# The modulation's columns for the first norm, summed in four groups of the array side by side instead of two

## The chip, the cores and the metric

The kernel runs on one core of one Trainium2 chip. The metric is the device time of one execution in microseconds (us); lower is better. Five engines work side by side on it: TensorE (PE in the profile, its weight loads PEld), VectorE (DVE), ScalarE (ACT), GpSimd (POOL) and SyncE (SP), which here issues the large transfers.

## What is computed

The reference is a transformer block with adaptive normalisation, sparse attention and a mixture of experts, followed by a second block. The change touches the first lines of the first block: the modulation vector `mod`, of which the first two sixths, the shift `sh1` and the scale `sc1`, go into the first norm.

```python
def first_block(x, c, ada_w, ada_b, ln1_g, ln2_g, w_in, ...):
    cond = jax.nn.silu(c)                                  # (1, 1024)
    for l in range(DEPTH):                                 # DEPTH = 1
        mod = (cond @ ada_w[l] + ada_b[l])[:, None, :]     # (1, 1, 6144)
        sh1, sc1, g1, sh2, sc2, g2 = jnp.split(mod, 6, axis=-1)
        h = rms_norm(x, ln1_g[l]) * (1.0 + sc1) + sh1      # x: (1, 512, 1024)
        x = x + g1 * hybrid_mixer(h, w_in[l], ...)
        ...
```

## The kernel before

512 tokens of width 1024 lie in four tiles of 128 tokens. After the first norm, `h` is needed turned, with its 1024 columns on the partitions in eight pieces `k` of 128, as the stationary operand of the product with `w_in` (`zchunk`, lines 257 to 259: three matmuls for each piece and token tile, since each operand is split in a high and a low part).

`start` makes `h` and begins this product. It works in four steps `jb` of 256 columns of `sc1` and `sh1`, that is of two pieces `k`. In a step, `ada(jb)` multiplies `cond` with two loaded blocks of `ada_w` (q = 0 for the scale, q = 1 for the shift, 8 x 128 rows by 256 columns, 1 MB each). `cond` stands 32 times over as the stationary operand, so a product takes 32 columns of the array and gives 32 equal rows. The products over `k` alternate between two 32-column groups of the array, groups 0 and 1 for q = 0 and groups 2 and 3 for q = 1, and so there are two partial sums for each q. Each of the 16 products of a step shows in the trace as two matmuls, 32 in all (line 468). ScalarE copies the bank to SBUF (line 472), `columns(jb)` turns it with TensorE (line 479) and adds up the two partial sums and the bias on VectorE (lines 483 to 490; the results are `A1` and `B1`, scale and shift by column), and `rows(jb)` turns the tokens (line 497), applies `A1` and `B1` on ScalarE (lines 499 and 500) and takes the low part on VectorE (line 501).

Step 0 runs ahead of the product with `w_in`. Steps 1 to 3 are hooks in it: `ada(jb)` is issued ahead of piece k = 2 jb - 2, `columns(jb)` and `rows(jb)` ahead of the next piece. The order on each engine is that of the code. The blocks are loaded by `Stream.pump` (line 135) on SP in the order in which they are used; they are split in a high part (line 167, ScalarE) and a low part (line 168, VectorE) if they belong to `w_in` or the experts. From 440 us on the weights of 32 experts (384 loads of 1 MB) stream through the same buffers.

Of the kernel before, what the change touches and what calls it, by code (L numbers as in the profile page):

```python
# [14 lines left out]
OP = mybir.AluOpType  # L15
AX = mybir.AxisListType
# [4 lines left out]
T = 512  # L21
NT = 4
D = 1024
KD = 8
# [163 lines left out]
class Build:  # L188
# [245 lines left out]
    def start(self):  # L434

        nc, I, st = self.nc, self.I, self.st
        mm = nc.tensor.matmul
        x = [self.xin[i // 2].v((i % 2) * D, D) for i in range(NT)]
        names = self.names = ["a0", "a1"]
        self.tb = self.sb = self.ring(names)  # L440
        pc = self.tb()
        nc.tensor.transpose(pc[:, :32], self.rows_a, self.ident[:32, :32])
        nc.vector.tensor_copy(self.cola, pc[:, :32])
        self.mb = self.ar.get()
        cond = self.mb.cols(0, 8)
        condr = self.condr = self.mb.v(256, KD, 32)
        nc.scalar.activation(cond, self.cola[:, 0:8], AF.Exp, scale=-1.0)
        nc.vector.tensor_scalar(cond, cond, 1.0, None, op0=OP.add)
        nc.vector.reciprocal(cond, cond)
        nc.vector.tensor_tensor(out=cond, in0=cond, in1=self.cola[:, 0:8], op=OP.mult)  # L450
        nc.vector.tensor_copy(condr, cond[:, :, None].to_broadcast([P, KD, 32]))
        sc = self.ar.get()
        A1, B1 = self.small(8, "A1", 1), self.small(8, "B1", 1)
        self.hT = [self.ar.get(F32R) for _ in range(4)]
        hH, hL = self.views(self.hT[:2]), self.views(self.hT[2:])
        self.hv = (hH, hL)

        sums = {}

        def ada(jb):  # L460

            pa = self.bank("a3")
            for q in range(2):
                u = self.u_ada1[jb][q]
                v = st.view(u)
                for k in range(KD):
                    o = 64 * q + 32 * (k % 2)
                    mm(pa[o:o + 32, 0:256], lhsT=condr[:, k, :], rhs=v[:, k, :], start=(k < 2), stop=(k >= KD - 2),
                       tile_position=(0, o))
                st.free(u)  # L470
            r = sums[jb] = sc.cols(D + 256 * (jb % 2), 256)
            nc.scalar.copy(r, pa[:, 0:256])

        def columns(jb):

            r = sums.pop(jb)
            pb = self.bank("a2")
            for j in range(2):
                nc.tensor.transpose(pb[:, j * P:(j + 1) * P], r[:, j * P:(j + 1) * P], self.ident)
            rows = self.small(8, "ab")  # L480
            p3 = pb[:, 0:256].rearrange("p (j g c) -> p j g c", j=2, g=4)[:, :, :, 0]
            r3 = rows.rearrange("p (j g) -> p j g", j=2)
            nc.vector.tensor_copy(r3, p3)
            s = slice(2 * jb, 2 * jb + 2)
            t = self.small(4, "abt")
            nc.vector.tensor_tensor(out=t[:, 0:2], in0=r3[:, :, 0], in1=r3[:, :, 1], op=OP.add)
            nc.vector.tensor_tensor(out=t[:, 2:4], in0=r3[:, :, 2], in1=r3[:, :, 3], op=OP.add)
            nc.vector.tensor_tensor(out=t[:, 0:2], in0=t[:, 0:2], in1=self.cola[:, 24 + 2 * jb:26 + 2 * jb], op=OP.add)
            nc.vector.tensor_tensor(out=B1[:, s], in0=t[:, 2:4], in1=self.cola[:, 16 + 2 * jb:18 + 2 * jb], op=OP.add)
            nc.vector.scalar_tensor_tensor(A1[:, s], t[:, 0:2], 1.0, self.cola[:, 8 + 2 * jb:10 + 2 * jb], op0=OP.add,  # L490
                                           op1=OP.mult)

        def rows(jb):
            for kk in (2 * jb, 2 * jb + 1):
                px = self.tb()
                for i in range(NT):
                    nc.tensor.transpose(px[:, i * P:(i + 1) * P], x[i][:, kk * P:(kk + 1) * P], self.ident)
                hf = sc.cols((kk % 2) * T, T)
                nc.scalar.activation(hf, px, AF.Identity, bias=B1[:, kk:kk + 1], scale=A1[:, kk:kk + 1])
                nc.scalar.copy(hH(kk), hf)  # L500
                nc.vector.tensor_tensor(out=hL(kk), in0=hf, in1=hH(kk), op=OP.subtract)

        def hook(k):
            jb = k // 2 + 1
            if jb < 4:
                if k % 2 == 0:
                    ada(jb)
                else:
                    columns(jb)
                    rows(jb)  # L510

        ss = self.small(NT, "ss")
        for i in range(NT):
            nc.scalar.activation(sc.cols(0, D), x[i], AF.Square, accum_out=ss[:, i:i + 1])
        nc.vector.tensor_scalar(ss, ss, 1.0 / D, EPS, op0=OP.mult, op1=OP.add)
        ri = self.rsqrt(ss, NT, "ri")
        for i in range(NT):
            if i % 2:
                nc.scalar.mul(x[i], x[i], ri[:, i:i + 1])
            else:  # L520
                nc.vector.tensor_scalar(x[i], x[i], ri[:, i:i + 1], None, op0=OP.mult)
        ada(0)
        columns(0)
        rows(0)

        self.cc = self.ar.get()
        c0, n, ids = self.z_chunks[1]
        self.weave(self.zchunk(self.hv, ids, n, lambda i, ps: self.z_evac(1, i, ps), hook=hook), thunks=0)
        self.ar.put(sc, *self.xin)
# [1904 lines left out]
```

## Time and profile before

| | us |
|---|---|
| median of 3 runs | 1750.85 |
| lowest and highest | 1750.61, 1752.01 |
| profiled execution, its own time | 1751.53 |
| its span in the trace | 1749.8 |
| TensorE busy in it | 1641.9 (94%) |
| VectorE, ScalarE, GpSimd busy | 1100.6, 847.0, 383.4 |
| first matmul of the modulation (line 468) | starts at 12.71 |

How the views read: a row of the timeline has its start, its length (from the first start to the last end), engine, line, operation, what it writes and reads, shapes and how many instructions are merged; in brackets stand the idle time ahead of it and what ended that. A row of the lines view has a group's count, its busy time and the mean ns of one. A row of the windows view has the stretch, its length, the busy time of each engine with the instructions in brackets, then TensorE's granted clock (1.00 is 2.4 GHz, 0.50 is 1.2 GHz), the share of the DMA engines' time and their GB/s. A row of the waits view has the time waited, how often, and the longest. In a merged row the last matmul ends later than it stops feeding the array, since matmuls are pipelined.

### The profile page before, as it was taken

The numbers are of one execution on the slowest core, as the hardware profiler recorded it, in microseconds if no ns is written. First come the engines' busy times: TensorE is split into PE (matmuls) and PEld (weight loads), VectorE is DVE, ScalarE is ACT, GpSimd is POOL, SyncE is SP. The second block draws the span as 40 slices with busy tenths as digits, with TensorE's granted clock in tenths as the row PEclk, the third lists the DMA queues.
The fourth block names the chain that finished last, engine by engine and source line by source line (L and its number), as shares of the span: only waits on it lengthen the run. The fifth ranks groups of instructions, "written<-read, shape, count | busy, mean of one in ns | idle before, by whom it ended". The sixth has DMA issues, their size and how long they took to land. (4 is left out here: it accounts for less than half of the span.)

```text
span 1749.8 us, 22154 instructions
## 1 busy us (share of the span) xinstructions
PE 1641.9 (94%) x7957; PEld 1059.2 (61%) x7958; DVE 1100.6 (63%) x1741; ACT 847.0 (48%) x1321; POOL 383.4 (22%) x259
## 2 busy tenths in 40 slices
PE   6999998898899999999999999999999989999998
PEld 3677764576765664564554454455455446778887
DVE  2567668668875575575475485476476486476653
ACT  4346568525554354264254254245245254477571
POOL 3012225223010120320320321231232130210120
PEclk9999999998999999999999999999999999999999
DMA  9712035456899999999999999999999986100301
GB/s 363 300 52 73 1 135 182 153 224 262 317 365 419 406 416 416 406 415 418 410 415 420 409 418 418 409 417 419 410 417 419 409 353 247 49 25 25 121 1 48
DMA packets 100007, 506.53 MB, mean 289 GB/s; under 512 B 10962, under 2 KB 20258, under 8 KB 48690
## 3 DMA queue, kind: packets, MB, share of 16 engines
q1 hardware_dynamic: 89972, 477.94, 67.1%
q0 software_dynamic: 9296, 26.07, 5.4%
q8 instruction: 64, 1.05, 0.2%
q10 hardware_dynamic: 624, 1.06, 0.2%
q14 instruction: 51, 0.42, 0.1%
HBM read 487.19 MB, written 17.84 MB: 289 GB/s over the span
## 5 line engine op out<-in xcount | busy, mean ns | idle before, releaser
L168 DVE TENSOR_TENSOR b<-b,b 128x1024 fp32r<-128x1024 f32 (+1 forms) x474 | 557.2, 1221 | 266.0 <-ACT b L167 265.3
L167 ACT CAST b<-b 128x1024 fp32r<-128x1024 f32 (+1 forms) x476 | 472.1, 1044 | 205.6 <-DMA b<-in_exp_w 163.5
L1739 POOL DMA_INDIRECT accd<-b,isc x16 | 162.3, 10146 | 431.0 <-DVE b L1734 431.0
L257 PE MATMUL z<-b,b 128*128 128x512 f32 (+1 forms) x544 | 225.0, 414 | 2.9 <-ACT b L167 2.1
L257 PE MATMUL u<-b,b 128*96 128x512 f32 (+1 forms) x560 | 224.7, 401 | 0.0
L259 PE MATMUL u<-b,b 128*96 128x512 f32 (+1 forms) x560 | 220.0, 393 | 0.0
L258 PE MATMUL u<-b,b 128*96 128x512 f32 (+1 forms) x560 | 219.7, 392 | 0.0
L1592 PE MATMUL u<-b,b 128*64 128x512 f32 x960 | 216.8, 597 | 1.4 <-DMA b<-in_exp_w 1.3
L258 PE MATMUL z<-b,b 128*128 128x512 f32 (+1 forms) x544 | 210.7, 387 | 1.5 <-DVE b L168 1.5
L259 PE MATMUL z<-b,b 128*128 128x512 f32 (+1 forms) x544 | 210.4, 387 | 0.0
L1592 PEld LDWEIGHTS u<-b,b 128*64 128x64 f32 x960 | 64.6, 136 | 123.0 <-issue 113.2
L258 PE MATMUL y<-b,b 128*96 128x512 f32 (+1 forms) x256 | 107.6, 420 | 21.0 <-DVE b L168 19.5
L257 PEld LDWEIGHTS z<-b,b 128*128 128x128 f32 x544 | 103.1, 190 | 33.5 <-issue 13.4
L257 PE MATMUL y<-b,b 128*96 128x512 f32 (+1 forms) x256 | 105.3, 411 | 17.5 <-ACT b L167 17.5
L257 PEld LDWEIGHTS u<-b,b 128*96 128x96 f32 (+1 forms) x560 | 96.1, 172 | 37.3 <-ACT b L167 5.7
L259 PEld LDWEIGHTS z<-b,b 128*128 128x128 f32 x544 | 102.7, 189 | 21.8 <-DVE b L1931 0.4
L259 PEld LDWEIGHTS u<-b,b 128*96 128x96 f32 (+1 forms) x560 | 95.8, 171 | 33.0
L258 PEld LDWEIGHTS u<-b,b 128*96 128x96 f32 (+1 forms) x560 | 96.1, 172 | 30.5
L258 PEld LDWEIGHTS z<-b,b 128*128 128x128 f32 x544 | 103.3, 190 | 16.2 <-DVE b L168 2.5
L1611 ACT CAST b<-tr 128x768 fp32r<-128x768 f32 (+1 forms) x33 | 28.6, 867 | 163.9 <-PE tr L1609 163.9
L1592 PE MATMUL y<-b,b 128*64 128x512 f32 x480 | 107.6, 600 | 0.0
L259 PE MATMUL y<-b,b 128*96 128x512 f32 (+1 forms) x256 | 103.5, 404 | 0.0
(516 smaller groups left out, 2101.4 us busy)
## 6 DMA issues: line engine op xcount, KB each, us to landing
b<-in_exp_w SPq DMA_DIRECT2D x384, 1024.0 KB, 19.5
b<-in_ada_w SPq DMA_DIRECT2D x24, 1024.0 KB, 8.8
b<-in_w_in SPq DMA_DIRECT2D x24, 1024.0 KB, 11.5
b<-in_w_out SPq DMA_DIRECT2D x8, 1024.0 KB, 5.2
b<-in_x SPq DMA_DIRECT2D x8, 512.0 KB, 4.3
b<-in_nsa_cmp_w POOLq DMA_DIRECT2D x2, 1024.0 KB, 10.1
b<-modd SPq DMA_DIRECT2D x4, 512.0 KB, 5.5
accd<-b SPq DMA_DIRECT2D x4, 512.0 KB, 3.8
```

What stands on the lines that cost most here:

```text
L167: nc.scalar.copy(hv, s)
L168: (other or nc.vector).tensor_tensor(out=lv, in0=s, in1=hv, op=OP.subtract)
L257: mm(out, lhsT=ah, rhs=bh, start=first, stop=False)
L258: mm(out, lhsT=ah, rhs=bl, start=False, stop=False)
L259: mm(out, lhsT=al, rhs=bh, start=False, stop=last)
L1592: mm(out[o, :], lhsT=lhsT, rhs=rhs[:, h * 512:(h + 1) * 512], start=False, stop=last, tile_position=(0, 64 * h), skip_group_check=True)
L1611: nc.scalar.copy(H[:, :, 0:n], pv)
L1739: nc.gpsimd.indirect_dma_start(out=self.accd, out_offset=bass.IndirectOffsetOnAxis(ap=self.isc[0:m, c:c + 1], axis=0), in_=ys[0:m, :], in_ ...
```

## The change

The product over `k` now goes round all four groups for both q: product `k` takes group `k % 4`, and q picks the columns of the bank (0 to 255 or 256 to 511) instead of the groups. So there are four partial sums of two products each, in place of two of four products each, and the bank holds 512 columns. The copy by ScalarE takes 512 columns, the turn takes four matmuls, and one reduction on VectorE over the four groups replaces a copy and two additions.

```diff
                 for k in range(KD):
-                    o = 64 * q + 32 * (k % 2)
-                    mm(pa[o:o + 32, 0:256], lhsT=condr[:, k, :], rhs=v[:, k, :], start=(k < 2), stop=(k >= KD - 2),
-                       tile_position=(0, o))
+                    o = 32 * (k % 4)
+                    mm(pa[o:o + 32, q * 256:(q + 1) * 256], lhsT=condr[:, k, :], rhs=v[:, k, :], start=(k < 4),
+                       stop=(k >= 4), tile_position=(0, o))
                 st.free(u)
-            r = sums[jb] = sc.cols(D + 256 * (jb % 2), 256)
-            nc.scalar.copy(r, pa[:, 0:256])
+            r = sums[jb] = sc.cols(D + T * (jb % 2), T)
+            nc.scalar.copy(r, pa)
...
-            for j in range(2):
+            for j in range(4):
                 nc.tensor.transpose(pb[:, j * P:(j + 1) * P], r[:, j * P:(j + 1) * P], self.ident)
-            rows = self.small(8, "ab")
-            p3 = pb[:, 0:256].rearrange("p (j g c) -> p j g c", j=2, g=4)[:, :, :, 0]
-            r3 = rows.rearrange("p (j g) -> p j g", j=2)
-            nc.vector.tensor_copy(r3, p3)
             s = slice(2 * jb, 2 * jb + 2)
             t = self.small(4, "abt")
-            nc.vector.tensor_tensor(out=t[:, 0:2], in0=r3[:, :, 0], in1=r3[:, :, 1], op=OP.add)
-            nc.vector.tensor_tensor(out=t[:, 2:4], in0=r3[:, :, 2], in1=r3[:, :, 3], op=OP.add)
+            nc.vector.tensor_reduce(out=t, in_=pb.rearrange("p (j g c) -> p j g c", j=4, g=4)[:, :, :, 0], axis=AX.X,
+                                    op=OP.add)
```

The matmuls of line 468 keep their number and their place. On VectorE, in step 0 (`a` with a number is a bank of PSUM, `abt` the sums), this stood in a row before:

```order
L521 TENSOR_SCALAR b_79<-b_79,riy 128x1024
L483 COPY ab<-a_196 128x8
L486 TENSOR_TENSOR abt<-ab 128x2
L487 TENSOR_TENSOR abt<-ab 128x2
L488 TENSOR_TENSOR abt<-abt,cola 128x2
L489 TENSOR_TENSOR B_151<-abt,cola 128x2
L490 SCALAR_TENSOR_TENSOR A_150<-abt,cola 128x2
L501 TENSOR_TENSOR b_154<-b_149,b_152 128x512 x2
```

Now there are four instructions between the same neighbours instead of six, in this step and in the three after it:

```order
L517 TENSOR_SCALAR b_79<-b_79,riy 128x1024
L482 TENSOR_REDUCE abt<-a_196 128x4
L484 TENSOR_TENSOR abt<-abt,cola 128x2
L485 TENSOR_TENSOR B_151<-abt,cola 128x2
L486 SCALAR_TENSOR_TENSOR A_150<-abt,cola 128x2
L497 TENSOR_TENSOR b_154<-b_149,b_152 128x512 x2
```

On TensorE the stretch from the end of step 0 to the first product with `w_in` read like this before (the lines 497 of before are 493 now):

```order
L468 MATMUL a_174<-b_89,b_143 32x256 x8
L479 MATMUL a_196<-ident,b_149 128x128 x2
L497 MATMUL a_207<-ident,b_78 128x128 x2
L497 MATMUL a_207<-ident,b_79 128x128 x2
L497 MATMUL a_215<-ident,b_78 128x128 x2
L497 MATMUL a_215<-ident,b_79 128x128 x2
L468 MATMUL a_228<-b_93,b_143 32x256 x8
L468 MATMUL a_228<-b_95,b_143 32x256 x8
L257 MATMUL z_224<-b_135,b_152 128x512
```

It now reads:

```order
L468 MATMUL a_174<-b_89,b_143 32x256 x8
L479 MATMUL a_196<-ident,b_149 128x128 x4
L493 MATMUL a_206<-ident,b_78 128x128 x2
L493 MATMUL a_206<-ident,b_79 128x128 x2
L493 MATMUL a_214<-ident,b_78 128x128 x2
L493 MATMUL a_214<-ident,b_79 128x128 x2
L468 MATMUL a_227<-b_93,b_143 32x256 x8
L468 MATMUL a_227<-b_95,b_143 32x256 x8
L257 MATMUL z_223<-b_135,b_152 128x512
```

Nothing has moved but the two matmuls more at line 479; no engine's order differs otherwise.

## Rows read from the trace of the kernel before

**Rows 1.** The page, part 1: busy time of each engine.
```profile
PE 1641.9 (94%) x7957; PEld 1059.2 (61%) x7958; DVE 1100.6 (63%) x1741; ACT 847.0 (48%) x1321; POOL 383.4 (22%) x259
```

**Rows 2.** Windows: the opening, the dense part behind it, the experts.
```profile
12.60:18.80 6.20, 6.02 (x32) 2.60 (x32) 1.33 (x2) 2.12 (x3) 3.16 (x6) 1.00 1.07 376
18.80:29.40 10.60, 5.68 (x44) 3.16 (x44) 3.41 (x10) 5.31 (x8) 0.00 (x0) 1.00 1.08 386
29.40:113.00 83.60, 81.69 (x507) 56.38 (x507) 41.35 (x122) 30.18 (x55) 12.01 (x13) 1.00 0.65 246
...
440.00:1440.00 1000.00, 953.39 (x4253) 546.91 (x4255) 627.54 (x620) 446.90 (x480) 221.34 (x60) 0.99 1.00 407
```

**Rows 3.** Timeline of TensorE, 12 to 42 us.
```profile
12.71 6.02 PE L468 MATMUL a<-b,b 128*32 128x256 f32 x32 [7.87 <-DMA b<-in_ada_w]
...
19.48 1.04 PE L497 MATMUL a<-ident,b 128*128 128x128 f32 x8
22.12 1.92 PE L468 MATMUL a<-b,b 128*32 128x256 f32 x16 [1.60 <-DMA b<-in_ada_w]
24.78 1.92 PE L468 MATMUL a<-b,b 128*32 128x256 f32 x16 [0.74 <-DMA b<-in_ada_w]
28.12 0.50 PE L257 MATMUL z<-b,b 128*128 128x512 f32 x1 [1.42 <-ACT b L167]
29.38 0.50 PE L258 MATMUL z<-b,b 128*128 128x512 f32 x1 [0.76 <-DVE b L168]
...
35.65 0.39 PE L259 MATMUL z<-b,b 128*128 128x512 f32 x1
35.96 2.82 PE L468 MATMUL a<-b,b 128*32 128x256 f32 x32
38.71 0.50 PE L257 MATMUL z<-b,b 128*128 128x512 f32 x1
...
41.57 0.38 PE L479 MATMUL a<-ident,b 128*128 128x128 f32 x2
```

**Rows 4.** Timeline of TensorE's weight loads (PEld) in step 0.
```profile
16.03 0.19 PEld L468 LDWEIGHTS a<-b,b 128*32 128x32 f32 x4 [0.57 <-DMA b<-in_ada_w]
```

**Rows 5.** Lines of TensorE: line 468 in 12.6 to 16, then 22 to 27.
```profile
L468 PE MATMUL a<-b,b 128*32 128x256 f32 x16 | 3.6, 632 | 7.9 <-DMA b<-in_ada_w 7.9
...
L468 PE MATMUL a<-b,b 128*32 128x256 f32 x32 | 3.8, 381 | 2.3 <-DMA b<-in_ada_w 2.3
```

**Rows 6.** Timeline of TensorE at 67.5 us: the four-group form, eight matmuls of 512 columns.
```profile
67.57 1.06 PE L641 MATMUL a<-b,b 128*32 128x512 f32 x8
```

**Rows 7.** Timeline of ScalarE behind step 1.
```profile
26.75 0.37 ACT L472 COPY b<-a 128x256 f32<-128x256 f32 x1 [3.46 <-PE a L468]
27.02 1.99 ACT L167 CAST b<-b 128x1024 fp32r<-128x1024 f32 x2
```

**Rows 8.** Lines of ScalarE, 28 to 140 us, shapes apart.
```profile
L567 ACT COPY b<-z 128x512 f32<-128x512 f32 x4 | 2.3, 586 | 5.8 <-PE z L259 5.7
```

**Rows 9.** Lines of VectorE, 18 to 70 us.
```profile
L588 DVE TENSOR_REDUCE vk<-b 128x8 f32<-128x512 f32 x1 | 0.7, 685 | 0.0
...
L483 DVE COPY ab<-a 128x8 f32<-128x8 f32 x4 | 0.7, 167 | 8.9 <-PE a L479 8.9
```

**Rows 10.** Timeline of TensorE at 445 us.
```profile
444.80 0.63 PE L257 MATMUL u<-b,b 128*128 128x512 f32 x1
445.22 0.63 PE L258 MATMUL u<-b,b 128*128 128x512 f32 x1
```

**Rows 11.** Windows: stretches around changes of the clock.
```profile
442.00:447.70 5.70, 5.50 (x14) 4.00 (x15) 5.04 (x6) 2.94 (x4) 0.00 (x0) 0.50 0.45 178
...
745.00:748.00 3.00, 0.52 (x2) 0.21 (x2) 1.30 (x2) 1.99 (x2) 0.00 (x0) 1.00 1.02 431
748.00:751.50 3.50, 3.50 (x9) 2.76 (x10) 3.41 (x4) 3.42 (x4) 0.00 (x0) 0.51 1.01 426
```

**Rows 12.** Waits of the SP queue, 300 to 440 us.
```profile
SPq L135 <- DVE b L168: 52.4, 9, 30.5
```

## The prediction

> **What bounds the kernel now.** Read the busy times first: TensorE is busy 94% of the span, no other engine over 63% [rows 1]. Then the windows [rows 2]: in the opening (12.6 to 29.4 us) the DMA engines are full (shares 1.07 and 1.08) and TensorE is busy 5.68 of 10.60 us in its second part; from 29.4 to 113 us TensorE is busy 81.69 of 83.60 us with the transfers at 0.65; the experts (440 to 1440 us) have TensorE at 953 of 1000 us and the DMA engines at 1.00. So the change sits where the kernel goes from waiting for loads to being dense on TensorE, and what counts is when the dense part begins and how long it is. The timeline [rows 3] tells how the opening ends: step 0 (12.71) and both blocks of step 1 (22.12 and 24.78) wait for a transfer of `ada_w`; the first product with `w_in` waits for line 167 (28.12) and its second for line 168 (29.38); from there no wait over 0.4 us until steps 2 (35.96) and 3 (the same row, at 45.50) are done. In step 0 the second block comes at 16.03 [rows 4].
>
> One more thing is to be read, TensorE's clock. Its column says 1.00 for the opening [rows 2], but the matmuls of line 468 take 632 ns on the mean from 12.6 to 16 us and 381 ns from 22 us on [rows 5]: the engine starts at the lower level (1.2 GHz) and rises to 2.4 GHz between, after it worked 6.02 of 6.20 us in step 0 [rows 2].
>
> **The change part by part.** *A burst.* Sixteen matmuls of one block take 1.92 us, of which the last is 0.38 [rows 3]: eight in each of two groups, so seven steps in 1.54, 0.22 us a step. Over four groups there are four in each: 3 x 0.22 + 0.38 = 1.04 us, 0.88 less. That four groups do work side by side is in the trace: line 641 does eight matmuls of 512 columns over four groups in 1.06 us, where one after the other on two groups the four steps of 0.44 would take over 1.7 [rows 6]. In steps 2 and 3 both blocks are there, and the 32 matmuls take 2.82 us, since the second block's groups already overlap the first's; eight in each of four groups give 7 x 0.22 + 0.38 = 1.92, 0.90 less in each of the two steps.
>
> *Step 0* gains and loses nothing that lasts: step 1 waits for its transfer at 22.12 whatever step 0 does [rows 3].
>
> *Step 1, the path.* Its second block arrives at 24.78. Before, the burst ends at 26.70, line 472 copies 256 columns in 0.37 us, and line 167 follows at 27.02 [rows 7], ahead of the dense part. A copy of 512 columns by ScalarE takes 0.59 us [rows 8], so +0.21 here. In steps 2 and 3 the longer copy stands between TensorE's burst and work that is needed one piece later, and costs nothing.
>
> *Turns.* Two matmuls more in each of four steps, at (1.04 - 0.27) / 7 = 0.11 us each (0.27 us is the last one's tail, estimated from line 479's row of two, 0.38 - 0.11) [rows 3]; in step 0 they lie before a wait, in steps 1 to 3 on the dense engine: 6 x 0.11 = +0.66.
>
> *VectorE.* A reduction takes the place of a copy and two additions. Nothing shows a reduction of 16 numbers; it lies between the 0.17 us of the copy of eight and the 0.69 of a reduction of 512, and I take 0.2, near the small one [rows 9]. The two further turns hold it up by 0.22, one dependent instruction less gives about 0.2 back, and `A1` and `B1` come as before. Even 0.69 lies beside some 12 products with `w_in` in steps 1 to 3 (35.65 is the last of them) and costs nothing.
>
> So far, at the upper clock: step 1 -0.88 + 0.21, turns +0.66, steps 2 and 3 -1.80, together -1.81 us.
>
> *The clock.* This sum takes the upper clock for granted. At the lower one a matmul takes 0.63 us [rows 5], and a step, at half the rate, 0.44: a four-group burst takes 3 x 0.44 + 0.63 = 1.95 us. Step 0 then runs from 12.71 to 14.66, waits for its second block until 16.03 [rows 4], and ends at 17.98. Before, it had no such gap: at half the array's width the first block lasted until the second came. The changed opening is bursts of 1.95 us and turns of some 2.8 us with waits between them, up to the dense part. Wherever the trace shows the clock going from 0.50 to 1.00, the engine had worked nearly unbroken: 6.02 of 6.20 us [rows 2], 5.50 of 5.70 us from 442.0, 3.50 of 3.50 us from 748.0 [rows 11]. And where it stood idle (0.52 us of work in 745.0 to 748.0) the clock fell right behind [rows 11]. I take it that the clock stays at the lower level until the dense part has run for a while: between 3.5 us (748.0 to 751.5) and 5.7 us (442.0 to 447.7), 4.6 in the middle. A product with `w_in` then takes 0.42 us [rows 10] instead of (41.57 - 38.71) / 12 = 0.24 [rows 3], so 0.18 x 4.6 / 0.42 = +2.0 us, with ends 1.5 and 2.4. Step 1's second burst is 1.95 instead of 1.92, so its -0.88 becomes +0.03.
>
> The Trainium skill bears on this place (TensorE: Matmul & The Clock Gate, "HAM oscillation — how this bites in real kernels"): bursts that are short against the transfer waits between them send the clock down, and the work should be laid so that the engine isn't left idle. That rule speaks against this change, which shortens the bursts and not the waits. By that rule the sum would be the one with the clock's term, without it the -1.81 above.
>
> Sum: +0.03 + 0.21 + 0.66 - 1.80 + 2.0 = **+1.1 us**, from 0.6 to 1.5 by the clock's ends.
>
> *What becomes of it.* From 29.4 us TensorE is dense, so all of it moves on. The first experts' loads wait for buffers that line 168 frees (52.4 us in nine waits of SP) [rows 12], so the transfers that fill 440 to 1440 us begin later by the same amount. I carry it whole; the other end is that the full DMA engines swallow it.
>
> The profiled execution took 1751.53 us, its span 1749.8 and 1.7 around it; with +1.1 it would be 1752.6. It lies 0.7 above the median of the three runs, 1750.85, and against that I forecast **1752.0 us**.
>
> **The rivals.** *The clock rises all the same,* in the turns of step 0 or by what the engine did before the trace begins to show it, and holds as it held before with TensorE busy 5.68 of 10.60 us [rows 2]. For it: that half-idle stretch did keep the upper level. Against: in the changed kernel the same stretch would hold about 10 x 0.11 + 0.27 + 0.22 for the turns, 2 x 1.04 and 0.5, some 4.2 of 10.6 us, and the rise must come first. Then -1.81: 1749.0 us.
>
> *Four groups don't work side by side here,* as all products of a block share one moving block. Then only the costs are left, 0.21 + 0.66 = +0.9: 1751.7. Against it stands line 641, which runs this very form [rows 6].
>
> *Slower, by a lower clock further on.* At 748.0 the engine had waited for lines 167 and 168, the clock fell, and 3.5 us were at 0.51 [rows 11]: at 0.18 of 0.42 us that is 1.5 us lost. Further starts of experts wait in the same way and keep the clock. If the shift by one microsecond brings two or more of them under, that decides it: 1.1 + 2 x 1.5 = +4.1, 1755.0. Against it: in the experts the transfers are full and may hide such a loss [rows 2]. The mirror of it, two such falls less on top of the first rival, gives 1749.0 - 3.0 = 1746.0.
>
> **How the numbers follow.** The forecast has 0.60, the rise all the same 0.22, no overlap 0.04, the further falls 0.08, fewer falls 0.06. A measurement of this kernel can tell about 0.2%, 3.5 us, from no change: under 1747.35 is faster, over 1754.35 slower. Only the last two cases lie outside, so faster 0.06, same 0.86, slower 0.08. For the range: the forecast's own is 1751.4 to 1752.4, with the three runs' spread of 1.4 around it, and the carry's lower end is 1750.85; the first rival is at 1749.0. From 1748.6 to 1753.7 takes in all but the last two cases and edges of the others.
>
> **What would show it.** In step 0 the row of line 468 splits in two with a gap up to 16.03, and line 468's mean is still over 600 ns in step 1, with bursts of 1.95 us; then the clock's step is right. Means near 380 ns there and bursts of 1.04 say the first rival. Line 257 first starts near 28.35; the products behind 29.6 are 0.42 apart until 33 to 35 us and 0.23 after. Steps 2 and 3 are rows of 32 in 1.9 us; 2.8 would say that the groups don't overlap. A dense part that begins 0.7 earlier with the clock up, or an end that doesn't follow the opening's shift, makes the prediction wrong.

## The result, and the profile after

The changed kernel takes **1762.62 us** (median of 4 runs, 1761.52 to 1762.99) against 1751.43 us (median of 4) for the kernel before: ratio 1.0062, 95% interval 1.0050 to 1.0074. It is slower by about 11 us. The forecast was 1752.0 us, and its range ended at 1753.7. The profiled execution of the changed kernel took 1761.52 us, its span is 1759.8.

The busy times answer to [rows 1], part 1 of the page of the kernel after:

```profile
PE 1648.0 (94%) x7965; PEld 1066.5 (61%) x7966; DVE 1101.4 (63%) x1733; ACT 849.3 (48%) x1321; POOL 382.4 (22%) x259
```

They tell nothing of 10 us: ScalarE has 2.3 us more, VectorE 0.8, and TensorE 6.1, which at 94% of a longer span says little.

The opening is told by the timeline of TensorE in the kernel after (columns as in [rows 3]):

```profile
13.48 1.93 PE L468 MATMUL a<-b,b 128*32 128x256 f32 x16 [8.15 <-DMA b<-in_ada_w]
16.46 1.94 PE L468 MATMUL a<-b,b 128*32 128x256 f32 x16 [1.05 <-DMA b<-in_ada_w]
19.10 1.11 PE L479 MATMUL a<-ident,b 128*128 128x128 f32 x4 [0.71 <-ACT b L472]
...
22.40 1.75 PE L468 MATMUL a<-b,b 128*32 128x256 f32 x16 [0.47 <-DMA b<-in_ada_w]
25.32 1.07 PE L468 MATMUL a<-b,b 128*32 128x256 f32 x16 [1.18 <-DMA b<-in_ada_w]
28.04 0.80 PE L257 MATMUL z<-b,b 128*128 128x512 f32 x1 [1.65 <-ACT b L167]
...
30.32 0.63 PE L257 MATMUL z<-b,b 128*128 128x512 f32 x1
30.75 0.63 PE L258 MATMUL z<-b,b 128*128 128x512 f32 x1
...
34.12 0.60 PE L479 MATMUL a<-ident,b 128*128 128x128 f32 x4
...
36.13 0.39 PE L257 MATMUL z<-b,b 128*128 128x512 f32 x1
36.35 0.39 PE L258 MATMUL z<-b,b 128*128 128x512 f32 x1
...
38.26 1.93 PE L468 MATMUL a<-b,b 128*32 128x256 f32 x32
...
47.12 1.93 PE L468 MATMUL a<-b,b 128*32 128x256 f32 x32
```

Step 0 is two bursts of 1.93 us with a wait between them, the products with `w_in` start 0.43 us apart and later 0.22, and steps 2 and 3 take 1.93 us instead of 2.82. That is the opening as forecast, but for step 1's second burst, which took 1.07 us where 1.95 was said. So the next question is where in the span the 10 us arise. Each matmul of one trace can be paired with the same matmul of the other. The one of the kernel after comes 1.0 us later at 65 to 112 us (forecast 1.1), 0.5 earlier at 127, 0.04 later from 460 to 600. From there on it falls behind steadily: 0.9 us at 628, 2.2 at 764, 4.4 at 1024, 6.5 at 1221, 9.8 at 1440, and 9.8 to the end. The whole loss lies between 600 and 1440 us, in the experts, where the change altered no instruction.

The windows answer to [rows 2]:

```profile
12.60:18.80 6.20, 3.87 (x32) 1.27 (x32) 1.75 (x4) 2.53 (x3) 3.34 (x7) 1.00 1.08 361
18.80:29.40 10.60, 6.53 (x46) 3.90 (x46) 3.30 (x8) 5.43 (x8) 0.00 (x0) 0.90 1.10 343
29.40:113.00 83.60, 81.75 (x505) 56.81 (x506) 39.81 (x113) 30.67 (x55) 12.01 (x13) 0.97 0.72 256
...
440.00:1440.00 1000.00, 956.63 (x4237) 552.26 (x4239) 618.98 (x613) 441.07 (x474) 220.37 (x60) 0.98 1.01 405
```

Read the last two columns. The share of the DMA engines' time is as high as before or higher, and in the three stretches where it is full the GB/s are lower: 361 for 376, 343 for 386, 405 for 407. (In the dense part, where it is not full, both are higher: 0.72 for 0.65, and 256 for 246.) In the full stretches the engines are as busy and carry less. The DMA view from 700 to 1400 us says it again, first of before, then of after (packets, MB and mean rate; then the queue of the large loads with its packets, MB and share of the 16 engines' time):

```profile
DMA packets 42871, 289.97 MB, mean 414 GB/s; under 512 B 4861, under 2 KB 4861, under 8 KB 9437
...
q1 hardware_dynamic: 37564, 273.56, 92.9%
```

```profile
DMA packets 42533, 287.48 MB, mean 411 GB/s; under 512 B 4826, under 2 KB 4826, under 8 KB 9402
...
q1 hardware_dynamic: 37226, 271.07, 93.0%
```

The same share for 0.9% fewer packets: each takes longer. In the records of the single packets, those of 8192 bytes on this queue (some 33,000 in this stretch) take 310.5 ns on the mean before and 313.7 after. One expert load is 128 such packets, eight for each DMA engine. In the kernel before 79 of the 384 loads have started by 600 us, where the matmuls aren't behind yet. The other 305 are 2440 packets an engine, and 2440 x 3.2 ns = 7.8 us, an estimate. The loads' own starts, paired in the same way, are 8.4 us behind at the last one (1417 us), and so are the matmuls up to 1430 us. So the longer packets account for most of the 9.8 us; the last 1.4 arise between 1430 and 1440 us, behind the start of the last load, and no run shows what they are.

The same view of 10 to 60 us, where the loads of `ada_w` come in packets of 1024 bytes (before, then after; the second line has the transfers' count, size and median us to landing):

```profile
DMA packets 13182, 19.41 MB, mean 388 GB/s; under 512 B 730, under 2 KB 9335, under 8 KB 12935
...
b<-in_ada_w SPq DMA_DIRECT2D x10, 1024.0 KB, 11.2
```

```profile
DMA packets 13092, 17.56 MB, mean 351 GB/s; under 512 B 723, under 2 KB 9567, under 8 KB 13078
...
b<-in_ada_w SPq DMA_DIRECT2D x10, 1024.0 KB, 13.9
```

Here the rate is a tenth lower; packets of 1024 bytes take 46.3 ns before and 50.8 after. A packet pays 3 ns more at the one size and 4.5 at the other.

### The profile page after: what moved, and what is told of

Its sections match the earlier page's. It is cut to its first block, busy times and chain, and to the rows that moved or that the text cites. A ratio compares the mean times of both kernels' runs of the same rounds, so it can differ in the third digit from the quotient of the medians.

```text
span 1759.8 us, 22162 instructions
## 1 busy us (share of the span) xinstructions
PE 1648.0 (94%) x7965; PEld 1066.5 (61%) x7966; DVE 1101.4 (63%) x1733; ACT 849.3 (48%) x1321; POOL 382.4 (22%) x259
## 3 DMA queue, kind: packets, MB, share of 16 engines
q8 instruction: 64, 1.05, 0.2%
q10 hardware_dynamic: 624, 1.06, 0.2%
## 5 line engine op out<-in xcount | busy, mean ns | idle before, releaser
L257 PE MATMUL y<-b,b 128*96 128x512 f32 (+1 forms) x256 | 109.3, 427 | 21.3 <-ACT b L167 21.3
L258 PE MATMUL y<-b,b 128*96 128x512 f32 (+1 forms) x256 | 111.4, 435 | 16.7 <-DVE b L168 15.6
L258 PEld LDWEIGHTS u<-b,b 128*96 128x96 f32 (+1 forms) x560 | 95.9, 171 | 30.6
L259 PE MATMUL y<-b,b 128*96 128x512 f32 (+1 forms) x256 | 107.9, 421 | 0.0
```

The source lines that it names most:

```text
L257: mm(out, lhsT=ah, rhs=bh, start=first, stop=False)
L258: mm(out, lhsT=ah, rhs=bl, start=False, stop=False)
L259: mm(out, lhsT=al, rhs=bh, start=False, stop=last)
```

## The experiments

**What was suspected.** `ab`, the tile of eight numbers that the change gave up, has two buffers, 64 bytes of each partition, and its pool lies ahead of the 25 blocks of 8 KB that take all large loads. By the compiled programs' allocation the blocks start at byte 24320 of each partition before, which is 95 x 256, and at 24256 after, 192 bytes behind a multiple of 256. Theory A: the place of the blocks lengthens the packets. Rival B: the clock; in the trace of after it falls 17 times, before 11 times. Rival C: something of the four-group form.

**The changed kernel with its blocks put back.**

```diff
+        self.pool("gap").tile([P, 16], F32, name="gap", bufs=1)
         ar = self.ar = Arena(self.pool("arena"), NB)
```

> The changed kernel with 64 unused bytes of each partition ahead of the 25 blocks of 8 KB, so that these lie where they lay before (from byte 24320 of the partition, a multiple of 256, instead of 24256). Theory A (the place of the blocks): the tile of 64 bytes that the change gave up moved every block, and transfers to a block that starts off a multiple of 256 take some 1% longer a packet; then this kernel takes 1751 to 1753 us, its 8192-byte packets take 310 to 311 ns again in the experts instead of 314, and the rate there is 414 GB/s instead of 411. Rival B (the clock): the shifted opening brought more starts of experts under the lower clock (17 falls instead of 11), and these cost the time; then the place changes nothing and this kernel stays at 1762. Rival C (the four-group form itself costs the time, in a way that the opening does not show): 1762 as well, with packets of 314 ns.

**The kernel before with its blocks moved.** The same line in the kernel before, with 16, 32, 48 and 8 numbers (64, 128, 192 and 32 bytes).

> The kernel before, with its code as it was and 64 unused bytes ahead of the blocks: they start 64 bytes behind a multiple of 256. Theory A says slower, about 1760 to 1762 us if every start off the multiple costs the same, and about 1754 to 1755 if the loss goes with the distance from it (64 of 192 bytes, a third of 10 us), with packets of 314 or of 311.5 ns. Rivals B and C: no part of the opening is changed, so 1751 us and packets of 310 to 311 ns.

> The kernel before with 128 unused bytes ahead of the blocks: they start 128 bytes behind a multiple of 256, but on a multiple of 128. Theory A with a step of 256: 1758 to 1762 us. Theory A with a step of 128: 1751 us, as before. Rivals B and C: 1751 us.

> The kernel before with 192 unused bytes ahead of the blocks: they start 192 bytes behind a multiple of 256, as in the changed kernel. Theory A: the whole loss without any part of the change in the code, 1760 to 1762 us, packets of 314 ns, 411 GB/s in the experts. Rivals B and C: 1751 us, 414 GB/s.

> The kernel before with 32 unused bytes ahead of the blocks. The loss was the same for 64, 128 and 192 bytes off a multiple of 256 (10.1, 10.1 and 10.7 us against the kernel before); if it is one further piece of each packet that costs, it is the same for 32: 1760 to 1763 us, packets of 313 to 314 ns. If the blocks' place counts only in steps of 64, 1751 us.

Measured; each beside runs of the kernel before on the same chip, the packets being those of 8192 bytes from 700 to 1400 us:

| kernel | blocks start behind a multiple of 256 by | median us | ratio, 95% interval | packet, ns | GB/s |
|---|---|---|---|---|---|
| before | 0 | 1751.43 | | 310.5 | 414 |
| after | 192 | 1762.62 | 1.0062, 1.0050 to 1.0074 | 313.7 | 411 |
| after, blocks put back | 0 | 1751.55 | 1.0002, 0.9992 to 1.0013 | 310.5 | 414 |
| before, moved by 32 | 32 | 1763.20 | 1.0061, 1.0044 to 1.0078 | 314.5 | 409 |
| before, moved by 64 | 64 | 1761.88 | 1.0060, 1.0045 to 1.0076 | 313.5 | 411 |
| before, moved by 128 | 128 | 1761.82 | 1.0056, 1.0040 to 1.0071 | 313.3 | 411 |
| before, moved by 192 | 192 | 1762.44 | 1.0062, 1.0047 to 1.0077 | 313.6 | 411 |

(The kernel before took 1751.43 us beside the kernel after, 1751.29 beside the one moved by 32 bytes, and 1751.77 beside the other four.) The place alone makes the whole difference, in both directions and without any part of the change's code. B and C, which expected 1762 for the changed kernel with its blocks put back and 1751 for the moved ones, are out. The moved kernels' traces have 16, 16, 19 and 13 falls of the clock (32, 64, 128 and 192 bytes) for the same loss. That the loss would grow with the distance is out too: 32 bytes cost as much as 192.

**Is a coarser multiple better still?** The small tiles' pool goes behind the blocks, which then start at 20480.

```diff
-        self.sm = self.pool("small")
...
+        self.pool("gap").tile([P, 32], F32, name="gap", bufs=1)
         ar = self.ar = Arena(self.pool("arena"), NB)
+        self.sm = self.pool("small")
```

> The kernel before with the pool of small tiles behind the blocks instead of ahead of them, so that the blocks start at byte 20480, a multiple of 4096 and not only of 256. Theory A with a step of 256: the same as before, 1751 to 1752 us, packets of 310 to 311 ns. If a coarser step counts too (512, 1024, 2048 or 4096): faster, by several us.

1750.77 us, ratio 1.0004 (0.9994 to 1.0013), packets 310.5 ns: nothing beyond 256.

**Half of the blocks moved.**

```diff
+        self.mid = None
...
         i = self.free.popleft()
         n = 4096 if dt == BF else 2048
+        if i == 12 and not self.mid:
+            self.mid = self.pool.tile([P, 16], F32, name="mid", bufs=1)
```

> The kernel before with 64 unused bytes between its twelfth and thirteenth block: blocks 0 to 11 start on multiples of 256, blocks 12 to 24 64 bytes behind one, and about half of the loads in the experts (231 of 448 transfers with an address set at run time) go to the latter. Theory A (each transfer to a block off the multiple takes about 1% longer by itself): half of the loss, 1756 to 1757.5 us, with 8192-byte packets of 312 ns on the mean in the experts. Rival D (what counts is that any block is off, as by the alignment of the whole stream or the falls of the clock it sets off): 1760 to 1762 or 1751.

1757.22 us against 1750.85, ratio 1.0045 (1.0028 to 1.0061). By the medians that is 6 of the 10 us, where A expected it; by the ratio it is 8, and the interval reaches from half of the loss to the whole. But the mean packet from 700 to 1400 us is 311.0 ns and not the 312 that A expected: 0.5 more than before, not half of 3.1. Nor do the packets carry the time here: 0.5 ns on 2440 packets would be 1.2 us, and in the profiled execution (1755.01 us, the fastest of the four) the loads' starts lose 2.3 us from 646 to 1417 us. So it isn't a fixed price for each packet to a moved block, and what the rest of this kernel's time is stays open. Nor is the price fixed in the other kernels: with all blocks moved by 64 bytes a third of these packets still take 309 ns, the usual figure, while a third take 312 and an eighth 319. What a packet must meet to be lengthened stays open.

**The loads without TensorE.** In the large experts' products only the one of the two high parts is left, so that TensorE cannot be what bounds; the second kernel has the 64 bytes ahead of its blocks.

```diff
+    def mm1(self, out, ah, al, bh, bl, first, last):
+        self.nc.tensor.matmul(out, lhsT=ah, rhs=bh, start=first, stop=last)
...
-                            self.mm3(u[0:m, c * 512:(c + 1) * 512], xH[e][:, k, 0:m], xL[e][:, k, 0:m], H[:, 0, s],
+                            self.mm1(u[0:m, c * 512:(c + 1) * 512], xH[e][:, k, 0:m], xL[e][:, k, 0:m], H[:, 0, s],
                                      L[:, 0, s], False, k == KD - 1)
...
-                        self.mm3(y[0:m, s], aH[:, k, 0:m], aL[:, k, 0:m], H[:, 0, s], L[:, 0, s], False, k == KD - 1)
+                        self.mm1(y[0:m, s], aH[:, k, 0:m], aL[:, k, 0:m], H[:, 0, s], L[:, 0, s], False, k == KD - 1)
```

> The kernel before, in which each large expert's product leaves out the two products with a low part and keeps that of the high parts; TensorE loses some 470 us of work in the experts, which leaves the loads alone as their bound. It is there to be compared with the same kernel with displaced blocks. Loads alone would need about 950 us at 309 ns a packet for what takes 1000 now, so 1700 to 1750 us are expected here by all theories; packets of 309 to 311 ns.

> The same with 64 unused bytes ahead of the blocks. Theory A (the transfers themselves are slower): with TensorE out of the way the loads show it whole, 8 to 11 us more than the kernel with the same products left out and blocks on the multiple, packets 3 to 4 ns longer. Rival D (TensorE waits more and its clock falls more often, and buffers come free later): with TensorE nearly half idle its clock no longer sets the end, so under 2 us of difference.

1741.98 us and 1751.86 us: 9.9 us between them, packets of 310.4 and 313.5 ns. Their windows of the experts, first on the multiple, then off it:

```profile
440.00:1440.00 1000.00, 731.71 (x2743) 295.74 (x2743) 630.09 (x626) 444.02 (x483) 261.79 (x61) 0.85 1.00 407
```

```profile
440.00:1440.00 1000.00, 732.71 (x2705) 292.41 (x2705) 621.20 (x616) 440.00 (x478) 260.23 (x60) 0.85 1.01 406
```

TensorE is busy 732 us of 1000 in both and has the same mean clock, 0.85, and the loss is there whole. So the transfers themselves are slower, and the loss doesn't need the clock. That the further falls in the kernel after (B) come from waiting for them is likely and not shown by a run of its own. The pair shows a second thing: 222 us less of TensorE's busy time in the experts (953.39 in [rows 2]; 470 less were expected, and what is left runs at the mean clock of 0.85) give only 9 us. And they give it early: against the kernel before, the loads of the first of the two start 7.8 us earlier at 581 us and 7.9 at 1356. So TensorE's work still counts up to about 580 us, and behind that the loads bound the experts, although TensorE is busy 95% of the time. That agrees with the kernel after beginning to fall behind at 600 us and not at 440. The windows of the kernel before have the DMA engines' share under 1 ahead of 600 us and full behind:

```profile
440.00:600.00 160.00, 157.80 (x712) 105.30 (x714) 114.25 (x110) 80.51 (x84) 18.57 (x9) 0.98 0.94 374
```

```profile
600.00:1440.00 840.00, 795.59 (x3543) 441.61 (x3541) 513.30 (x510) 366.39 (x396) 202.77 (x51) 0.99 1.01 413
```

**Does the opening reach the end?** The shifts of the opening in the five other executions (from -1.7 to +1.8 us at 65 us) seemed to be gone by the end, so a delay of known size was put into the dense part of the kernel before.

```diff
         def hook(k):
+            if k == 6:
+                px = self.tb()
+                for _ in range(24):
+                    mm(px, lhsT=hH(1)[:, 0:P], rhs=hH(0), start=True, stop=True)
             jb = k // 2 + 1
```

> The kernel before with 24 more products of 128 x 512 on TensorE ahead of piece 6 of the first product with w_in, where TensorE is dense: 24 x 0.23 = 5.5 us more in the opening, which the rows at 60 to 110 us should show whole. The prediction carried what the opening gains or loses whole to the end: then 1756 to 1757.5 us. Theory E (the experts' loads bound the kernel from about 440 us on, and their start does not follow the opening, since the shifts of the opening by -1.7 to +1.8 us in five executions were gone by the end): under 1.5 us are left, 1751 to 1752.5.

Its row in the lines of TensorE from 50 to 66 us:

```profile
L507 PE MATMUL a<-b 128*128 128x512 f32 x24 | 5.6, 389 | 0.0
```

1756.79 us against 1751.29, ratio 1.0027 (1.0016 to 1.0037): 5.5 us were put in, and 5.5 arrived by the medians, 4.7 (2.8 to 6.5) by the ratio. Theory E, with under 1.5, is out, and within that interval the prediction's carry was right. In the trace the pairs are 6.3 us later at 65 to 112 us, 4.7 from 127 and 4.4 at the end. The step at 113 to 127 us is a fall of the clock that the kernel before has there (in the window 113.0 to 116.6 us its clock is 0.53) and this execution has not. Such falls, of some 1.5 us each, come and go from one execution to another, and can hide an opening.

**The clock in the opening.** More matmuls behind the bursts of steps 0 and 1, on the changed kernel with its blocks put back, and then on the kernel before.

```diff
+                if jb < 2:
+                    spare = self.bank("a1")
+                    for k in range(16 if jb + q == 2 else 8):
+                        o = 32 * (k % 4)
+                        mm(spare[o:o + 32, 0:256], lhsT=condr[:, k % 8, :], rhs=v[:, k % 8, :], start=True, stop=True,
+                           tile_position=(0, o))
                 st.free(u)
```

> The changed kernel with its blocks on multiples of 256 again, and in the opening 8 more matmuls behind each of the first three blocks of line 468 and 16 behind the fourth, written to a bank that nothing reads: they fill the waits of TensorE for the next block of ada_w. Theory of the prediction (the clock stays at 1.2 GHz in the opening because of the waits between the bursts): the clock rises before step 1 and does not fall between 25 and 35 us, the bursts of step 1 take 1.04 to 1.07 us, the products with w_in are 0.23 apart from the first, and the opening ends 1.5 to 2 us ahead of the kernel before at 65 us. If the waits have nothing to do with it, the clock falls again at 27 to 31 us as in the changed kernel. For the end theory E says no difference either way, 1750.5 to 1752.5; if openings are carried, 1749 to 1750.

> The kernel before (two groups, its own blocks) with the same filler in the opening: 8 more matmuls in four groups behind each of the first three blocks of line 468, 16 behind the fourth. The changed kernel with this filler and its blocks on multiples of 256 took 1746.2 us against 1751.3 for the kernel before. If the four groups give 1.8 us once the clock is kept up, and an opening's gain is carried to the end, this kernel lies between, 1748 to 1749.5 us, with bursts of 1.92 us in step 1 and of 2.8 us in steps 2 and 3 and a shift of -0.5 to -1.2 us at 65 us. If the filler alone makes the difference, 1746 to 1747 us. If the filler does nothing for two groups, whose clock is up by 17 to 19 us in any case, 1750.5 to 1752.

Timeline of TensorE of the changed kernel with the filler (line 474):

```profile
12.92 1.93 PE L468 MATMUL a<-b,b 128*32 128x256 f32 x16 [7.73 <-DVE riy L273]
14.60 1.65 PE L474 MATMUL a<-b,b 128*32 128x256 f32 x16
16.07 1.05 PE L468 MATMUL a<-b,b 128*32 128x256 f32 x16
16.93 1.05 PE L474 MATMUL a<-b,b 128*32 128x256 f32 x16
...
21.01 1.07 PE L468 MATMUL a<-b,b 128*32 128x256 f32 x16 [1.57 <-DMA b<-in_ada_w]
...
23.72 1.07 PE L468 MATMUL a<-b,b 128*32 128x256 f32 x16 [0.77 <-DMA b<-in_ada_w]
24.61 1.91 PE L474 MATMUL a<-b,b 128*32 128x256 f32 x32
26.45 0.50 PE L257 MATMUL z<-b,b 128*128 128x512 f32 x1
...
28.27 0.39 PE L257 MATMUL z<-b,b 128*128 128x512 f32 x1
```

The second burst of step 0 is already at 1.05 us, those of step 1 at 1.07, and the products with `w_in` run at 0.39. From 29.4 to 113 us the clock is 1.00 throughout:

```profile
29.40:113.00 83.60, 81.68 (x528) 57.40 (x527) 41.60 (x124) 31.26 (x58) 12.00 (x13) 1.00 0.65 247
```

The pairs are 2.75 us ahead of the kernel before at 65 us, where 1.5 to 2 were expected; 1.06 of it is that step 1's second block came at 23.72 us here and at 24.78 before [rows 3]. The time is **1746.21 us** against 1751.29, ratio 0.9968 (0.9956 to 0.9981), where 1749 to 1750 was the least that was expected. So this version beats both kernels. The Trainium skill (TensorE: Matmul & The Clock Gate, "HAM oscillation — how this bites in real kernels") asks for work that doesn't leave the engine idle between short bursts; these rows agree with it. The kernel before with the same filler takes 1749.56 against 1750.57, ratio 0.9993 (0.9984 to 1.0002): no difference that can be told, just over the 1748 to 1749.5 that were expected. Its opening is not the expected one: at 65 us the pairs are 0.5 us behind, not 0.5 to 1.2 ahead. The clock fell from 21.3 to 24.8 us in spite of the filler, and 14 matmuls of step 1's first block took 3.20 us where 16 took 1.92 [rows 3]:

```profile
21.44 3.20 PE L468 MATMUL a<-b,b 128*32 128x256 f32 x14 [2.15 <-DMA b<-in_ada_w]
```

So the filler alone doesn't give the gain. That the four groups pay because it holds the clock is likely, but this pair doesn't show it, since the clock was not held in the trace of the second kernel. The two ratios are 0.25% apart, some 4 us, which is more than the 1.8 us that the bursts hold. In the trace of the version with the filler the pairs gain a further 1.55 us at 113 to 127 us and 1.6 near 320, where the kernel before has falls of the clock. Whether the filler keeps those away or one execution happened to lack them is open.

## Why the prediction was wrong, point by point

*What bounds the kernel.* Half right. That the DMA engines are full in the experts stood in [rows 2] and was said. But they were used only as a cover that might hide something ("the full DMA engines swallow it"), and never as the bound through which a change could cost. The pair with less of TensorE's work shows that they are the bound there, from about 580 us on.

*The change part by part.* **This is the step that failed.** The list of what the change removes held a copy and two additions, and not the tile `ab` that they worked on; with it everything allocated behind it moved by 64 bytes. ("Nothing has moved", ahead of the prediction, holds for the order of instructions and not for addresses.) So the place of the blocks stood in the sum at nothing, without a reason. In its place the runs showed 11 us, 1762.62 us with the blocks displaced and 1751.55 with them put back, most of it the 3.2 ns more a packet; the whole listed sum was +1.1. No row of the trace of before shows what a displaced block costs, and no bound for it was looked for. Without the displacement the forecast fits, 1751.55 us where 1752.0 was said, but that doesn't confirm its sum: the interval (0.9992 to 1.0013, -1.4 to +2.3 us) holds +1.1 and no change as well, and the trace of that run is at -1.7 and not at +1.1 at 65 us.

*The terms that were listed.* Their sizes came out, but for step 1's second burst. Bursts at the lower clock took 1.93 and 1.94 us (1.95 said), the burst of 32 1.93 (1.92 said), the turns 0.60 for four against 0.38 for two in the dense part [rows 3]. Line 472's copy takes 588 ns (0.59 said), and the reduction 175 (0.2 said):

```profile
L472 ACT COPY b<-a 128x512 f32<-128x512 f32 x4 | 2.4, 588 | 10.0 <-PE a L468 10.0
```

```profile
L482 DVE TENSOR_REDUCE abt<-a 128x4 f32<-128x16 f32 x4 | 0.7, 175 | 11.3 <-PE a L479 11.3
```

*The clock.* Right in its effect and too simple in its course. The second burst of step 1 took 1.07 us, so the clock had risen for a while; it fell again while the engine waited, and the first products ran at the lower level:

```profile
27.20:34.10 6.90, 5.60 (x12) 3.98 (x13) 2.36 (x2) 1.73 (x2) 0.00 (x0) 0.51 1.08 364
```

At 65 us this gave +1.0. That it is so near the forecast's +1.1 is partly luck: the burst took 0.88 us less than was reckoned, its block came 0.54 us later (25.32 for 24.78), and the lower level lasted to 34.1 us. Nor had the clock risen only behind nearly unbroken work in the trace of before, as was read there: from 403.4 to 410.2 us it was at 0.50 with TensorE busy 3.61 of 6.80 us, and rose then. And the fall isn't the change's alone. With its blocks put back the changed kernel had the clock down only from 28.2 to 31.7 us and stood at -1.7 at 65 us. That is near the first rival's -1.81 by luck too: the clock did fall, and step 1's second block had come 1.64 us earlier than before (23.14). And the kernel before, moved by 192 bytes, has such a fall as well, with products 0.43 apart, which the one trace at hand did not show:

```profile
30.60:34.00 3.40, 3.40 (x11) 2.62 (x10) 0.05 (x1) 0.00 (x0) 0.00 (x0) 0.50 1.07 369
```

When the opening's loads land and where the clock falls differs from one execution to the next, and one trace of before was taken for the rule.

*The carry* was right within what the delay could show: 5.5 us in, 4.7 (2.8 to 6.5) out.

*The rivals.* "Slower, by a lower clock further on" named the right stretch and a thing that can be seen there, 17 falls instead of 11, and put 1755.0 to it. Its mechanism is not the one: the pair with less of TensorE's work lost as much at one and the same mean clock. More likely the falls follow from slower loads. What speaks for that in the trace of after alone is where the loads' queue waits from 700 to 1100 us (for what, us in total, times, longest), before and after: longer for its own transfers, shorter for line 168, which frees buffers.

```profile
SPq L135 <- DMA b<-in_exp_w: 178.0, 120, 5.0
SPq L135 <- DVE b L168: 91.5, 65, 3.4
```

```profile
SPq L135 <- DMA b<-in_exp_w: 203.1, 123, 5.1
SPq L135 <- DVE b L168: 74.5, 61, 3.4
```

The range ended at 1753.7 because every case in it was about the opening, where the edit is.

## What to carry to other kernels

Read a diff for the tiles that it adds, drops or resizes, and look where the allocation puts everything behind them: here 64 bytes given up cost 10 us, and the edit could gain 1.8 by the prediction's own sum. In a stretch that the loads bound, keep the start of their buffers on a multiple of 256 bytes in the partition, by an unused tile if need be, and look at GB/s at an equal DMA share to see it. And an edit that shortens bursts between waits may need something that holds the clock: with blocks in place this one is no faster than before (ratio 1.0002), with the filler as well it is 0.3% faster.

## What the runs showed of the hardware

- A load to a buffer that doesn't start on a multiple of 256 bytes of the partition has longer packets: 313.3 to 314.5 ns on the mean instead of 310.5 for 8192 bytes, 50.8 instead of 46.3 for 1024, the same for 32, 64, 128 and 192 bytes off it; a multiple of 4096 is no better than one of 256. With half of the blocks off it the mean was 311.0 ns. The Trainium skill (DMA: Bandwidth & Descriptors, "How a descriptor splits into AXI transactions") says that a descriptor that doesn't start on a multiple of 256 bytes has its first transaction start at the boundary below, and that the bytes before its start still cost. The runs agree on the multiple, though the page speaks of what a transaction reads and the blocks here are written; by the beats that the page counts (an estimate from its table) the price would rise with the distance, and it doesn't.
- TensorE at 95% busy was not the bound: 222 us of its work taken out of 1000 gave 9 us, and nothing more behind 580 us.
- A fall of TensorE's clock outside the experts moves the pairs by some 1.5 us (113 to 127 us, and near 320), and which falls there are differs from one execution to the next, in the opening too: from 27.2 to 34.1 us in the kernel after, 28.2 to 31.7 with its blocks put back, 30.6 to 34.0 in the kernel before moved by 192 bytes, and none there in the kernel before.
